# Column mean of an 8192 x 8192 matrix: the loads moved to GpSimd's queue, one packet for each DMA engine, with TensorE announcing the landings

## The chip, the cores and the metric

One core of a Trainium2 chip. The metric is the device time of one execution in microseconds (us). The kernel before takes 627.35 us, the median of three runs (627.28 to 627.52).

The core has a tensor engine (TensorE, PE), a vector engine (VectorE, DVE), a scalar engine (ScalarE, ACT), GpSimd (POOL) and a sync engine (SyncE, SP). Each has its own instruction queue and can issue transfers (DMAs), which 16 DMA engines carry out. Engines tell each other of progress through counting semaphores; a DMA adds 16 to its semaphore when it has landed.

## The reference

```python
x = np.random.randn(8192, 8192).astype(np.float32)

def reference(x):
    return np.mean(x, axis=0)
```

268 MB are read once and 32 KB are written. The work is one addition for each number.

## The kernel before

The matrix has 8192 rows, 64 slabs of 128 rows; a slab fills the 128 partitions of on-chip memory with 32 KiB each. A **pair** is two slabs, 8 MiB (`C` is 8192 columns). 31 pairs (`n_pairs`, k = 0 to 30) are followed by two single slabs. The rows are dealt out so that each of the 128 partitions reads one contiguous run of 64 KiB for a whole pair (`source`, lines 79 to 84; which rows meet in a partition doesn't matter to a sum over all rows).

**Buffers.** There is room for three pairs (`bufs`, line 49). Pair k goes to buffer k % 3, so load k may start only when pair k - 3 has been used up.

**Loads** (lines 123 to 153). `cuts` (86 to 92) says in how many pieces a pair comes. Pair 0 comes in two, 1 MiB and 7 MiB, and both go out on ScalarE's queue. Every other load goes out on SP's queue: pairs 1 to 24 whole, pairs 25 to 29 in two halves, pair 30 in four quarters, then one slab in two halves (key `slab`) and the last slab in eight pieces, the last of them small (key `last`). Load 1 waits for `first`, the landing of the first MiB; load 2 stands behind it and waits for nothing else. From load 3 on, a pair's first piece waits until its buffer is free: for `freed` at least k - 2 while the loop runs, then for a count of VectorE's additions.

**Additions on VectorE.** Line 162 adds the two halves of pair 0 (its own fold). A loop of 8 rounds with 3 pairs each (lines 165 to 173) handles pairs 1 to 24 (`LOOPED`). For each pair it waits for the landing (168), adds the previous pair's running sum to the new pair's first half (169), tells that the previous buffer is free (170, `freed`), and adds the new pair's second half (171). So the sum moves from buffer to buffer, and buffer k - 1 becomes free in the middle of pair k. The semaphore `landed[b]` is reset by the vector engine itself: it subtracts 16 when the pair is consumed. Pairs 25 to 30 and the first slab are added by instructions written out one by one (lines 176 to 182).

**The end.** TensorE first waits until most additions are done (line 223), runs four matmuls that warm it up (225), and then sums over the 128 partitions by matmuls with ones (lines 189 and 201), the total and the last slab's pieces, into eight banks. ScalarE and VectorE scale the banks by 1/8192 (248, 251), and SP and ScalarE store the result (268, 282).

The order of work around the change is written by hand. An engine's queue is worked off in order, so a load that waits holds up the loads behind it on the same queue. Before the change TensorE's queue holds nothing ahead of line 223, and GpSimd's holds no load at all. The lines that matter most:

```python
168  nc.vector.wait_ge(landed[new], 16)
169  vadd(bufs[new][:, 0:C], bufs[old][:, 0:C]).wait_op(landed[old], 0, "sem-eq").then_inc(half, 1)
170  nc.vector.wait_ge(half, n + 1).then_inc(freed, 1)
171  vadd(bufs[new][:, 0:C], bufs[new][:, C : 2 * C]).then_inc(landed[new], -16)
```

Of the kernel before, what the change touches and what calls it, by code (L numbers as in the profile page):

```python
# [20 lines left out]
LOOPED = 24  # L21
# [3 lines left out]
def kernel(  # L25
# [5 lines left out]
    nc = tc.nc  # L31
# [47 lines left out]
    def source(k, lo, hi):  # L79
        if k < n_whole:  # L80
            b, t = divmod(k, RUN // 2)
            return blocks[b, :, 2 * t * C + lo : 2 * t * C + hi]
        j = lo // C
        return single(2 * (k - n_whole) + j, lo - j * C, hi - j * C)

    def cuts(k):
        if k == 0:
            return [(0, FIRST), (FIRST, 2 * C)]
        if k < n_pairs - BY_ROW:
            return [(0, 2 * C)]  # L90
        step = H if k == n_pairs - 1 else C
        return [(lo, lo + step) for lo in range(0, 2 * C, step)]

    with tc.tile_critical():  # L94
        sem = nc.alloc_semaphore
        landed = [sem(f"landed{b}") for b in range(3)]
        first, freed, half = sem("first"), sem("freed"), sem("half")
        dve, act, pe, stored = sem("dve"), sem("act"), sem("pe"), sem("stored")
        came = {}

# [19 lines left out]
            done.append(len(adds))  # L120


        def load(key, dst, src, after=None):

            ld = (nc.scalar if key[0] == 0 else nc.sync).dma_start(out=dst, in_=src)  # L125
            if after is not None:
                ld.wait_op(after[0], after[1], "sem-ge")
            if key not in came:
                came[key] = sem(f"came_{'_'.join(map(str, key))}")
            ld.then_inc(came[key], 16)  # L130

        for k in range(n_pairs):
            for n, (lo, hi) in enumerate(cuts(k)):
                after = None
                if k >= 3 and n == 0:
                    f = k - 3
                    after = (freed, f + 1) if f < LOOPED else (dve, freed_by[f])
                if k == 1:
                    after = (first, 16)
                key = (k, n)  # L140
                if k <= LOOPED:
                    came[key] = first if (k, n) == (0, 0) else landed[k % 3]
                load(key, bufs[k % 3][:, lo:hi], source(k, lo, hi), after)
        r = (n_slabs - 2) * P
        for n in range(2):
            after = (dve, freed_by[n_pairs - 3]) if n == 0 else None
            load(("slab", n), slab[:, n * H : n * H + H], single(n_blocks - 1, n * H, n * H + H), after)
        at, lo = {}, 0
        for n, w in enumerate(PIECES):
            load(("last", n), last[:, lo : lo + w], x[r + P : R, lo : lo + w])  # L150
            for c in range(lo, lo + w, 32):
                at[c] = came["last", n]
            lo += w
# [30 lines left out]


        n_pe = 0

        def mm(dst, src, **flags):
            return nc.tensor.matmul(out=dst, lhsT=ones, rhs=src, skip_group_check=True, **flags)  # L189
# [34 lines left out]
        for _ in range(4):  # L224
            nc.tensor.matmul(  # L225
                out=banks[7][:, 0:512], lhsT=idle[:, 0:P], rhs=idle, start=True, stop=True, skip_group_check=True
# [87 lines left out]
```

## Time and profile before

| | |
|---|---|
| median of three runs | 627.35 us |
| the profiled execution | 627.58 us |
| its span in the profile | 625.8 us |
| VectorE busy | 541.3 us, 86% |
| TensorE busy | 13.7 us, 2% |
| GpSimd busy | 0.2 us, 4 memsets |
| read from main memory | 268.44 MB, 429 GB/s over the span |
| one addition of 128 x 8192 numbers | 8.69 us |
| median of the loop's loads, issue to landing | 29.8 us |

The page cuts the span into 40 slices; for each it gives the busy share of every engine in tenths, the mean busy share of the 16 DMA engines (row "DMA") and the rate of transfer (row "GB/s"). A transfer's bytes are counted where its packet starts, so the rate swings between neighbouring slices where packets are long. The queues are listed with packets and bytes. The chain of waits starts at the last instruction and goes back, at each step, to what released it; a "DMA" in it is the time from a load's issue to its landing, which includes the time that the load spends behind others. The view of a tile's instructions gives the same time for chosen loads.

### The profile page before, as it was taken

To read this page: it belongs to the slowest core of one execution; us is meant where nothing else is said; L and a number is where in the kernel's file an instruction comes from. 1 tells how busy PE (TensorE), PEld (TensorE's weight loads), DVE (VectorE), ACT (ScalarE), POOL (GpSimd) and SP (SyncE) were. 2 spreads that over 40 slices of the span, in tenths; PEclk is the share of its full clock that TensorE was granted. 3 is DMA by queue.
4 is the path that set the end of the run, shared out by engine and by line. 5 is a ranking of instruction groups with operands and counts; after the bars stand their busy time and mean duration, and the time that the engine had idled before them with its cause. 6 is when DMAs were issued, how large, how long until landed. Compare 5 with 4: busy or idle time off the path is not lost.

```text
span 625.8 us, 467 instructions
## 1 busy us (share of the span) xinstructions
PE 13.7 (2%) x86; PEld 4.6 (1%) x86; DVE 541.3 (86%) x71; ACT 3.7 (1%) x6; POOL 0.2 (0%) x4
## 2 busy tenths in 40 slices
PE   0000000000000000000000000000000000000025
PEld 0000000000000000000000000000000000000011
DVE  0049999989888899888898888988889899999996
ACT  0000000000000000000000000000000000000001
POOL 0000000000000000000000000000000000000000
PEclk9999999999999999999999999999999999999999
DMA  9999999999999999999999999999999999999997
GB/s 380 433 461 402 469 402 469 402 469 402 469 402 461 411 452 419 448 423 406 465 402 469 402 469 402 469 402 469 402 469 402 434 429 425 431 425 436 435 429 312
DMA packets 7231, 268.48 MB, mean 429 GB/s; under 512 B 1069, under 2 KB 1329, under 8 KB 1470
## 3 DMA queue, kind: packets, MB, share of 16 engines
q1 hardware_dynamic: 6940, 260.08, 96.1%
q10 hardware_dynamic: 290, 8.39, 3.2%
q14 instruction: 1, 0.01, 0.0%
HBM read 268.44 MB, written 0.03 MB: 429 GB/s over the span
## 4 chain that ended last, share of the span: by engine, by line
DMA 59%; DVE 39%; issue 0%; SPq 0%; PE 0%; DVEq 0%; ACTq 0%
DMA pair<-in_x_dram 59%; DVE pair L157 39%; SPq L125 0%; PE bank L189 0%; DVE row L251 0%; ACTq L125 0%; DVEq L170 0%; DVEq L168 0%; DVEq L157 0%; ACTq L309 0%; SPq L94 0%
## 5 line engine op out<-in xcount | busy, mean ns | idle before, releaser
L157 DVE TENSOR_TENSOR pair<-pair 128x8192 f32<-128x8192 f32 (+1 forms) x32 | 269.6, 8426 | 42.4 <-DMA pair<-in_x_dram 38.7
L157 DVE TENSOR_TENSOR pair<-pair,pair 128x8192 f32<-128x8192 f32 (+2 forms) x35 | 270.1, 7717 | 35.5 <-DMA pair<-in_x_dram 35.0
L225 PE MATMUL bank<-idle 128*128 128x512 f32 x8 | 5.3, 818 | 605.5 <-DVE pair L157 605.5
L189 PE MATMUL bank<-pair,ones 128*32 128x512 f32 (+5 forms) x78 | 8.4, 523 | 3.7 <-DVE pair L157 3.6
L225 PEld LDWEIGHTS bank<-idle 128*128 128x128 f32 x8 | 2.1, 276 | 607.9 <-DVE pair L157 605.5
L248 ACT ACTIVATE rw<-bank 128x512 f32<-128x512 f32 x3 | 1.8, 597 | 617.2 <-PE bank L189 617.2
L251 DVE TENSOR_SCALAR r<-bank 128x352 f32<-128x352 f32 x1 | 0.5, 525 | 3.2 <-PE bank L189 3.2
L189 PEld LDWEIGHTS bank<-pair,ones 128*32 128x32 f32 x78 | 2.6, 108 | 10.2 <-DVE pair L157 7.1
L248 ACT ACT_TABLE_LOAD x1 | 1.3, 1283 | 1.8 <-issue 1.8
L159 DVE MEMSET ones<- 128x32 f32 x1 | 0.1, 85 | 1.0 <-SPq L94 1.0
L248 ACT ACTIVATE row<-bank 1x192 f32<-1x192 f32 (+1 forms) x2 | 0.6, 308 | 0.6 <-PE bank L189 0.6
L160 DVE MEMSET idle<- 128x512 f32 x1 | 0.5, 485 | 0.1
L251 DVE TENSOR_SCALAR row<-bank 1x288 f32<-1x288 f32 x1 | 0.4, 449 | 0.0
L298 POOL MEMSET const-bfloat16-1.0<- 128x1 bf16 x1 | 0.1, 102 | 0.0
L298 POOL MEMSET const-uint8-127<- 128x1 uint8 x1 | 0.1, 102 | 0.0
L298 POOL MEMSET const-float32-0.0<- 128x1 f32 x1 | 0.1, 99 | 0.2 <-issue 0.2
L298 POOL MEMSET const-float32-1.0<- 128x1 f32 x1 | 0.1, 99 | 0.0
## 6 DMA issues: line engine op xcount, KB each, us to landing
pair<-in_x_dram SPq DMA_DIRECT2D x10, 4096.0 KB, 27.6
pair<-in_x_dram SPq DMA_DIRECT2D x6, 2048.0 KB, 28.4
pair<-in_x_dram ACTq DMA_DIRECT2D x1, 7168.0 KB, 38.1
pair<-in_x_dram SPq DMA_DIRECT2D x3, 1024.0 KB, 33.4
pair<-in_x_dram ACTq DMA_DIRECT2D x1, 1024.0 KB, 4.7
pair<-in_x_dram SPq DMA_DIRECT2D x1, 704.0 KB, 36.6
pair<-in_x_dram SPq DMA_DIRECT2D x24, 29.8
pair<-in_x_dram SPq DMA_DIRECT2D x1, 144.0 KB, 30.2
```

The source lines that it names most:

```text
L157: return nc.vector.tensor_tensor(out=a, in0=a, in1=b, op=ADD)
L159: nc.vector.memset(ones, 1.0)
L160: nc.vector.memset(idle, 0.0)
L189: return nc.tensor.matmul(out=dst, lhsT=ones, rhs=src, skip_group_check=True, **flags)
L225: nc.tensor.matmul(out=banks[7][:, 0:512], lhsT=idle[:, 0:P], rhs=idle, start=True, stop=True, skip_group_check=True)
L248: op = engine.mul(out=dst, in_=src, mul=inv_r).then_inc(act, 1)
L251: op = engine.tensor_scalar(out=dst, in0=src, scalar1=inv_r, scalar2=None, op0=MULT).then_inc(dve, 1)
L298: nc = _bacc.Bacc("TRN2", target_bir_lowering=False, num_devices=1)
```

## The change

All loads except pair 0's two pieces go out on GpSimd's queue in place of SP's, with `single_packet=True`: a DMA engine's whole share of a load is framed as one packet. Their waits stay as they were.

The loads of pairs 1 to 24 now add to new semaphores, `count[b]`, one for each buffer, which only ever grow. TensorE waits for each of these 24 landings in turn and adds 16 to `landed[b]`, on which VectorE waits as before. Pair 0's 7 MiB still add to `landed[0]` directly. Pairs 25 to 30, the slab and the last pieces have semaphores of their own, as before. The 24 waits stand on TensorE's queue ahead of line 223.

```diff
+        count = [sem(f"count{b}") for b in range(3)]
...
         def load(key, dst, src, after=None):
-
-            ld = (nc.scalar if key[0] == 0 else nc.sync).dma_start(out=dst, in_=src)
+            if key[0] == 0:
+                ld = nc.scalar.dma_start(out=dst, in_=src)
+            else:
+                ld = nc.gpsimd.dma_start(out=dst, in_=src, single_packet=True)
             if after is not None:
                 ld.wait_op(after[0], after[1], "sem-ge")
...
                 if k <= LOOPED:
-                    came[key] = first if (k, n) == (0, 0) else landed[k % 3]
+                    came[key] = first if (k, n) == (0, 0) else landed[0] if k == 0 else count[k % 3]
                 load(key, bufs[k % 3][:, lo:hi], source(k, lo, hi), after)
...
         n_pe = 0
+        for k in range(1, LOOPED + 1):
+            nc.tensor.wait_ge(count[k % 3], 16 * (k // 3 + (k % 3 > 0))).then_inc(landed[k % 3], 16)
```

## The prediction

> **What bounds the kernel now.** I read the page's slices and queues first, then each load's landing, then the chain of waits at the start, because the change touches only loads and who announces them.
>
> ```profile
> span 625.8 us, 467 instructions
> ...
> DMA  9999999999999999999999999999999999999997
> GB/s 380 433 461 402 469 402 469 402 469 402 469 402 461 411 452 419 448 423 406 465 402 469 402 469 402 469 402 469 402 469 402 434 429 425 431 425 436 435 429 312
> ...
> q1 hardware_dynamic: 6940, 260.08, 96.1%
> q10 hardware_dynamic: 290, 8.39, 3.2%
> ```
>
> The transfer engines are busy in every slice. The swing between 402 and 469 is only the slicing of long packets. q1 is SP's queue and q10 is ScalarE's. ScalarE's two loads are 128 rows each, 256 rows, and its queue shows 290 packets: one packet for each row, and the rest are small entries such as the counts that announce a landing.
>
> The loads of pairs 1, 2 and 3, picked by their time of issue (instructions of the pair buffers in a narrow window; duration in ns, then first and last start in us, then time to landing):
>
> ```profile
> L125 SPq DMA_DIRECT2D pair<-in_x_dram x1: 387/387/387, 5.6 to 5.6; - x1
> ...
> DMA to landing us min/median/max: 36.2/36.2/36.2
> ```
> ```profile
> L125 SPq DMA_DIRECT2D pair<-in_x_dram x1: 411/411/411, 6.1 to 6.1; - x1
> ...
> DMA to landing us min/median/max: 55.1/55.1/55.1
> ```
> ```profile
> L125 SPq DMA_DIRECT2D pair<-in_x_dram x1: 328/328/328, 57.1 to 57.1; - x1
> ...
> DMA to landing us min/median/max: 23.5/23.5/23.5
> ```
>
> So pair 1 lands at 41.8, pair 2 at 61.2, pair 3 at 80.6; by the same view pairs 4, 5 and 6 at 99.8, 119.2 and 138.6. That is (138.6 - 41.8)/5 = 19.36 us for 8 MiB, or 433 GB/s. The fixed cost of a load that finds idle engines comes from the first one: 1 MiB (2.42 us at that rate) lands 4.7 us after its issue, so 2.3 us. Check: 2.3 + 268.44 MB at 433 GB/s (619.5) = 621.8; the last load lands at 621.5. The span is transfer time plus 4.3 us of closing work. VectorE needs 17.5 us a pair against 19.36 and waits. Its unbroken chain from 495 to 582 is no bound either: from its last release, at 582.7, 16 MiB are still to come, 38.7 us at the rate, and they end at 621.5.
>
> A full slice row does not mean that nothing can empty the engines. This is the start, in the chain of waits (start, us, what):
>
> ```profile
> 1.32 38.12 DMA pair<-in_x_dram
> ...
> 39.57 8.70 DVE pair L157
> ...
> 48.29 8.70 DVE pair L157
> ...
> 57.02 0.02 DVEq L170
> ```
>
> Pair 0 is folded at 39.57, pair 1 is added to it at 48.29, and at 57.02 L170 frees buffer 0 for load 3. Load 2 lands at 61.2. With three buffers nothing else can be issued: the engines run dry if buffer 0 comes free more than about 2 us (the fixed cost) after 59.
>
> **How two queues share the engines.** Pair 0's second load is 7 MiB, 16.9 us alone, yet it lands 38.1 us after its issue, when nearly 8 MiB of load 1 have come too. Rows of the two queues took turns, about one each. The queue view of short windows shows it at the end of that load. By 36.5 us all 8.39 MB of q10 have been started; between 36.5 and 38 q10 starts nothing, and between 36.5 and 39.5:
>
> ```profile
> q1 hardware_dynamic: 19, 1.25, 95.7%
> q10 hardware_dynamic: 13, 0.00, 0.2%
> ```
>
> The 13 entries without bytes are 13 of the load's 16 counts. Even a count waited for a whole row of the other queue (64 KiB on one of 16 engines, 2.4 us). A turn is one packet.
>
> **The change, part by part.**
>
> *Framing.* A load of 128 rows is 8 rows for each engine. One packet makes the turn 8 rows, 512 KiB, 19.4 us, in place of 2.4 us. After the start there is one queue only, and nobody to take turns with. At the start there is ScalarE's 7 MiB, 8 rows of 56 KiB for each engine, 2.1 us each. They start about 5 us in, after the first MiB. Load 1 still waits for `first` at 5.6; before, its rows could not come until a fixed cost later, and GpSimd's come about as late or a little later. By then ScalarE has had 2 or 3 rows and needs 5 or 6 and a count. It gets one turn between load 1 and load 2 (two if load 1's count is its own packet), and the remainder only behind load 2. So pair 0 lands last of the three, when all 24 MiB are there: at 61.2, where load 2 landed before (the same bytes, no gap), in place of 39.44.
>
> From there every step has a row. VectorE starts 0.13 later, at 61.3, as it did at 39.57. Buffer 0 is free 17.45 later (57.02 - 39.57), at 78.8. All three buffers are full until then, and the engines idle. Load 3 is issued, finds idle engines, and lands 0.05 + 2.3 + 19.36 later, at 100.5, against 80.6: **+19.9 us**. Does it come back? The engines are the bound, so lost transfer time stays lost. Is there a second gap? Buffer 1 is free at 61.3 + 35.0 = 96.3 and load 3 lands about 101: 4 to 5 us of cover for load 4's start. For load 5 it is 1.8 more (19.36 - 17.5), and so on. No.
>
> *GpSimd in place of SP.* No load of before is issued there, so its price is bounded by rows of the other queues. ScalarE's first load starts its issue at 0.90, and the engines move in the second microsecond; SP spends 0.33 to 0.43 on each. GpSimd may take from 0.4 less than SP to 2.3 more (the whole fixed cost again). I take 0.9 more, near ScalarE's time from issue to motion. It counts once, in load 3's gap: **+0.9**. Load 1's start lies beside ScalarE's 7 MiB. Loads 4 to 24 have 4 to 10.5 us of cover. The last ten loads follow the release at 582.7 with 8 MiB (19.4 us) still ahead of them; up to 3 us each they come in time. What is queued behind a waiting load on GpSimd is only later loads, in the same order as on SP, so nothing else is held up; SP's stores get an empty queue, but their data come after the last landing.
>
> *TensorE's relay.* One semaphore instruction for each of 24 landings, two hops in place of one; VectorE's own such steps (L168, L170) show 0.02 to 0.03 and 0.02 to 0.09 around them, so about 0.1 us. Landing to release of a buffer has 10.5 us of cover in the steady loop, and at pair 3 VectorE is late anyway: nothing. Behind the waits on TensorE stands only the closing work, which waits until 605.5; the last relay is over 100 us earlier. Without cover it would be 24 x 0.1 = 2.4 us.
>
> *Longer packets for the rate.* 19.36 us a load against 8 rows at 2.4 leaves no gap between loads that I can see; a gain by fewer packets is at most some tenths of a per cent, a loss per load anything from nothing to SP's 0.4. I take nothing.
>
> Sum: 19.9 + 0.9 = 20.8 us. Of the profiled execution (span 625.8, 627.58 in all): 646.6 and 648.4. On the median of 627.35: **648.2 us**.
>
> The Trainium skill, DMA: Bandwidth & Descriptors, section "Queues, rings and completion order", says that an engine drains a whole packet of one ring before it goes to another; by it the sum is the same 648. The same page, section "Issuing engines are not separate DMA queues", says that DMAs interleave whichever engine started them and that only issue time changes; by it alone nothing happens, which is the first rival. The one-row turns of before agree with both; no run here yet shows a packet of many rows.
>
> **Rivals.**
>
> *The turns stay short* (0.14), the side that is not slower: the arbiter still changes queue after a row, or the framing is not applied. For it: no row of before shows a long packet. Pair 0 then lands at about 39.5, and load 3 has its 4.2 us (57.0 to 61.2) less the 2.3 for its start: 1.9 us cover GpSimd's 0.9. Time 627.4, from 625.5 to 629. It decides wherever pair 0 lands before about 41.
>
> *Pair 0 gets through between loads 1 and 2* (0.06), because load 1 comes so late that ScalarE has one or two entries left, or turns are weighed by bytes. That needs load 1 to start after about 16 us, 10 after its release. Pair 0 lands at 2.3 + 2 x 19.36 = 41.0, load 3 at about 81.3: +0.7, 628.0. Also within no change.
>
> *VectorE keeps GpSimd from writing* (0.04): each load's release is followed at once by an 8.70 us add. If load 3's issue waits for its end, 8.7 more: 656.9; later loads then have 10.5 - 8.7 = 1.8 us, about enough. The Trainium skill, SBUF — State Buffer, section "Who interferes with whom", has such a lock, but for this add only against GpSimd's reads. No run here shows it yet.
>
> *A gap between packets on top of the forecast* (0.06): up to 0.4 us for each of some 30 loads, 12 us: up to 660.
>
> **Numbers.** The forecast has 0.70. Its own ends: GpSimd's price from -0.4 to +2.3, the start 1 us either way and a slight gain of rate give 645 to 651. The range leaves out the two rivals without change (0.20) and runs from the forecast's low end to 660. A difference under 0.2% (1.25 us) can't be told from no change here. Faster by more: 0.03, all from the first rival. Within: 0.15 (0.09 of the first, 0.06 of the second). Slower: 0.82 (0.70 + 0.04 + 0.06 + 0.02 of the first).
>
> **What would show it.** In the changed trace: pair 0's 7 MiB lands at about 61 in place of 39.4, after loads 1 and 2; VectorE's first add starts there; one or two of the first five slices show engines nearly idle (about 61 to 81), and all others 9; load 3 lands at about 101; from there landings 19.4 apart. If pair 0 lands at 40, framing does not act and the first rival holds; if later slices fall below 9 too, the price is per load; if load 3's issue lies 8.7 after its release, it is VectorE.

## The result and the profile after

The changed kernel takes 630.45 us (median of five runs, 630.34 to 630.59); the kernel before, with the same number of runs, takes 627.52 (627.28 to 627.81). The ratio is 1.0047, 95% interval 1.0033 to 1.0061: slower by 2.9 us, where 20.8 were forecast. The profiled execution took 630.39 us with a span of 628.4.

These lines of the page of the changed kernel answer to those shown of before:

```profile
span 628.4 us, 493 instructions
...
DMA  9999999999999999999999999999999999999995
GB/s 380 430 459 405 463 400 467 400 467 400 467 400 467 400 467 400 467 400 467 400 467 400 467 400 467 400 467 400 467 400 434 434 434 434 434 434 434 434 422 249
...
q0 software_dynamic: 6496, 260.05, 95.7%
```

q0 is GpSimd's queue. No slice shows idle engines, so the gap of the forecast isn't there. The start of the chain of waits shows why (start, us, what):

```profile
1.32 35.66 DMA pair<-in_x_dram
...
37.12 8.70 DVE pair L161
45.84 8.70 DVE pair L161
...
54.68 8.70 DVE pair L161
...
72.44 27.54 DMA pair<-in_x_dram
```

Pair 0's 7 MiB land at 37.0 (before: 39.4), not at 61, and buffer 0 is free at 54.6. By the times to landing (35.9, 54.7, 25.8 and 27.54 us from issues at 5.83, 6.50, 54.88 and 72.44) pairs 1 to 4 land at 41.7, 61.2, 80.7 and 100.0: before's landings within 0.2 us.

The view of the queues shows the turns. When ScalarE's last row starts (window 0 to 32.15 us), so much of load 1 has been started:

```profile
q0 software_dynamic: 80, 5.24, 37.6%
```

That is 80 rows of 64 KiB, 5 for each DMA engine. By the starts in the trace they alternate with ScalarE's last rows one by one: 2.4 us for a row of load 1, 2.1 for one of ScalarE's. In the kernel before it was 96 rows, 6 for each: there load 1's first row started at 9.1 us, here only at 11.1. One row less, 2.4 us, is why pair 0 now lands 2.4 us earlier. At the other end:

```profile
585.62 35.89 DMA pair<-in_x_dram
621.51 0.04 issue
621.55 1.42 PE bank L195 x11
```

621.51 is where before's chain has its last landing too. It is that of the last wide piece, 704 KB; the four narrow pieces land up to 622.5, in both kernels. The last computing instruction, VectorE's at 622.97, starts where it did (622.98). The whole difference in span lies after the work. It is in the view of line 94, which is where the hand-ordered section (`tc.tile_critical`) closes; of before and of after (duration in ns, first and last start in us):

```profile
L94 SPq NOP  x2: 13/13/13, 0.7 to 625.0; - x2
L94 DVEq DRAIN  x1: 10/10/10, 623.6 to 623.6; - x1
L94 PEldq DRAIN  x1: 8/8/8, 623.6 to 623.6; - x1
L94 SPq DRAIN  x1: 407/407/407, 623.6 to 623.6; - x1
...
L94 ACTq DRAIN  x1: 8/8/8, 625.0 to 625.0; - x1
```
```profile
L94 SPq NOP  x2: 13/13/13, 0.7 to 627.6; - x2
L94 POOLq DRAIN  x1: 3986/3986/3986, 623.6 to 623.6; - x1
L94 DVEq DRAIN  x1: 10/10/10, 623.6 to 623.6; - x1
...
L94 ACTq DRAIN  x1: 8/8/8, 625.0 to 625.0; - x1
```

Every engine that took part in the section drains its queue at its end, and SP's NOP marks that all have. Before, ScalarE is last at 625.0, after its wait for the stores. Now GpSimd takes part too, and its drain takes 3986 ns, from 623.55 to 627.54; everything behind it is 2.6 us later. That is the 2.6 us of span. GpSimd has issued its last load by 588.3, but its drain waits, like TensorE's and VectorE's, for a signal that SP gives behind the issue of its last store (622.97 to 623.47 here); in every run these drains begin 0.1 us behind that issue, but for GpSimd's where a drain of its own (below) still runs. SP's own drain takes 0.4 us in both kernels, after 51 transfers issued and after 3. Another 0.2 us lie outside the span (630.39 - 628.4 against 627.58 - 625.8).

### The profile page after: what moved, and what is told of

Same layout as the page of the kernel before. It is cut to its first block, busy times and chain, and to the rows that moved or that the text cites. A ratio compares the mean times of both kernels' runs of the same rounds, so it can differ in the third digit from the quotient of the medians.

```text
span 628.4 us, 493 instructions
## 1 busy us (share of the span) xinstructions
PE 13.7 (2%) x86; PEld 4.6 (1%) x86; DVE 541.2 (86%) x71; ACT 3.7 (1%) x6; POOL 25.6 (4%) x52
## 3 DMA queue, kind: packets, MB, share of 16 engines
q0 software_dynamic: 6496, 260.05, 95.7%
## 4 chain that ended last, share of the span: by engine, by line
DMA 63%; DVE 35%; issue 1%; POOL 0%; PE 0%; PEldq 0%; DVEq 0%; ACTq 0%; SPq 0%
DMA pair<-in_x_dram 63%; DVE pair L161 35%; POOL pair L129 0%; PE bank L195 0%; PEldq L192 0%; DVE row L257 0%; ACTq L127 0%; DVEq L174 0%; DVEq L172 0%; DVEq L161 0%; ACTq L315 0%; SPq L94 0%
## 5 line engine op out<-in xcount | busy, mean ns | idle before, releaser
L129 POOL DMA_DIRECT2D pair<-in_x_dram x48 | 25.4, 532 | 562.4 <-DVEq L174 476.0
## 6 DMA issues: line engine op xcount, KB each, us to landing
pair<-in_x_dram ACTq DMA_DIRECT2D x1, 7168.0 KB, 35.7
pair<-in_x_dram POOLq DMA_DIRECT2D x1, 704.0 KB, 35.9
pair<-in_x_dram POOLq DMA_DIRECT2D x24, 29.4
```

What stands on the lines that cost most here:

```text
L129: ld = nc.gpsimd.dma_start(out=dst, in_=src, single_packet=True)
```

## The experiments

**Theory:** the 2.6 us are GpSimd's drain, and it is long because of the loads that GpSimd issued. **Rivals:** the drain costs 4 us whenever GpSimd takes part; a fixed price for any load; TensorE's relay carries the loss. Beside it stood the question why framing changed nothing in the turns.

**No load on GpSimd, but it takes part** (the kernel before):

```diff
+        nc.gpsimd.wait_ge(first, 16)
```

> The kernel before, with one semaphore wait added on GpSimd inside the section and no load there; nothing of the computation changes. Theory: the changed kernel's 2.6 us of span lie in GpSimd's drain at the section's end (3986 ns, from 623.55), and the drain is long because loads went through GpSimd. Then this drain takes under 0.1 us and the time is before's, 627.3 to 627.8. Rival: every engine that takes part in the section has to drain at its end, and GpSimd's drain takes 4 us whatever it did; then 3.9 to 4.0 us of drain and 630.2 to 630.6.

Measured: ratio 1.000 (0.9989 to 1.001), 627.65 us. The view of line 94:

```profile
L94 POOLq DRAIN  x1: 41/41/41, 624.0 to 624.0; - x1
```

Taking part costs nothing; the loads make the drain long.

**One load on GpSimd:**

```diff
+            elif key[0] != 1:
+                ld = nc.sync.dma_start(out=dst, in_=src)
...
-        for k in range(1, LOOPED + 1):
+        for k in (1,):
             nc.tensor.wait_ge(count[k % 3], ...)
```

> Only load 1 on GpSimd (framed, relayed by TensorE), all others on SP. Theory by number: the drain goes through the loads that GpSimd issued, 3.99 us for 48 or 0.08 each; with one load it takes 0.1 to 0.3 us and ends before ScalarE's wait for the stores, so 627.3 to 627.8. Rival, fixed: the first use of the drain after any GpSimd load costs 4 us (its code is fetched, for example); then 3.9 us and 630.2 to 630.6.

Measured: ratio 1.0269 (1.0248 to 1.0289), 644.5 us, not the time expected, but the drain came out as the theory by number has it:

```profile
L94 POOLq DRAIN  x1: 130/130/130, 640.7 to 640.7; - x1
```

The 17 us are of my making. Load 2 has no wait of its own; it stood behind load 1's wait on one queue. Left on SP, it went out at 0.96 and shared the engines with pair 0 from the start. Pair 0's first MiB, in rows of 8 KiB, took turns with rows of 64 KiB and landed 25.2 us after its issue in place of 4.7, and load 1 went out only at 26.4. Pair 0's second part, which then took turns with load 1, landed at 57.6 (56.2 us after its issue at 1.4), and load 1 last of the three, at 62.3. The table of stretches (us; busy time of PE, PEld, DVE, ACT, POOL; granted clock, DMA share, GB/s, both counted where a packet starts) shows the engines run dry:

```profile
55.00:60.00 5.00, 0.00 (x0) 0.00 (x0) 2.31 (x1) 0.00 (x0) 0.00 (x0) 1.00 0.97 419
60.00:65.00 5.00, 0.00 (x0) 0.00 (x0) 5.00 (x1) 0.00 (x0) 0.00 (x0) 1.00 0.00 0
...
75.00:80.00 5.00, 0.00 (x0) 0.00 (x0) 4.86 (x2) 0.00 (x0) 0.00 (x0) 1.00 1.06 406
```

So the kernel fell by accident into the state that the forecast had described: all buffers full, VectorE starting late (57.69), no transfers for some 14 us, from 62.1 to 76.2. Load 3 goes out at 75.2, and its view ends with:

```profile
DMA to landing us min/median/max: 22.7/22.7/22.7
```

So it lands at 97.9.

**The loop's 24 loads on GpSimd, the later 24 on SP:**

```diff
+            elif key[0] not in range(1, LOOPED + 1):
+                ld = nc.sync.dma_start(out=dst, in_=src)
```

> Loads 1 to 24 on GpSimd, the 24 later ones on SP. Theory by number: half the drain, 1.9 to 2.1 us from 623.55 to 625.6, about 0.6 us past the 624.99 at which before's section ends: 627.9 to 628.4. Fixed: 3.9 us, 630.2 to 630.6.

Measured: ratio 1.0054 (1.0034 to 1.0074), 631.05 us, again not the time expected, but the drain is as the theory by number has it:

```profile
L94 SPq NOP  x2: 13/16/18, 0.7 to 628.7; - x2
L94 POOLq DRAIN  x1: 2016/2016/2016, 626.6 to 626.6; - x1
...
L94 ACTq DRAIN  x1: 8/8/8, 628.0 to 628.0; - x1
```

The drain ends 0.6 us behind ScalarE, as expected, but it begins 3.1 us later than in the changed kernel. Where the loads change queues, load 24 on GpSimd's queue takes turns with load 25 on SP's, and lands 33.0 us after its issue where its predecessor took 29.4. VectorE starts pair 24 late, has no slack from there to the end, and finishes its last addition at 622.57, 3.3 us later than before.

**A drain of its own behind the last load:**

```diff
+        nc.gpsimd.drain()
```

> The changed kernel with a drain of its own on GpSimd, right behind the last load's issue, so that GpSimd waits for its loads there and not at the section's end. Theory by number: the drain goes along with the landings and ends with the last of them, about 621.6 to 622.0; the drain at the section's end finds nothing left, under 0.2 us; time as before, 627.3 to 627.9. Rival, fixed per drain: the last drain takes 4 us again, 630.2 to 630.6. Third: the work on the 48 loads begins only when the last has landed, then it ends about 4 us after 621.9 and the gain is 1.5 us or so, 628.6 to 629.2.

Measured: ratio 1.0004 (0.9994 to 1.0014), 627.91 us, no difference from before. The two drains:

```profile
L160 POOLq DRAIN  x1: 37501/37501/37501, 586.9 to 586.9; - x1
```
```profile
L94 SPq NOP  x2: 13/13/13, 0.7 to 624.9; - x2
...
L94 POOLq DRAIN  x1: 41/41/41, 624.5 to 624.5; - x1
```

The section's own drain is back at 41 ns and the loss is gone, which shows the cause by mending it. The early drain ends at 624.4, 2.0 us after the last landing (622.4) and not with it. That lies between the first expectation and the third: some of its work is done only after the last landing, but it ends ahead of ScalarE (624.9). In what order it goes through the loads stays open.

**More loads, the same bytes:** pairs 25 to 30 cut twice as fine, 62 loads on GpSimd.

```diff
-        step = H if k == n_pairs - 1 else C
+        step = H // 2 if k == n_pairs - 1 else H
```

> The changed kernel with the pieces of pairs 25 to 30 cut in half: 62 loads on GpSimd in place of 48, the same bytes. The drain took 41 ns with no load, 130 with one, 2016 with 24 and 3986 with 48, about 82 for each. By number: 0.04 + 62 x 0.082 = 5.1 us, 1.15 more at the end: 631.5 to 631.8. If the drain goes by bytes or by packets in place of loads (these stay or grow by less than a fifth), 4.0 to 4.4 us and 630.4 to 630.9.

Measured: ratio 1.0097 (1.0067 to 1.0126), 633.52 us.

```profile
L94 POOLq DRAIN  x1: 5129/5129/5129, 626.0 to 626.0; - x1
```

5129 ns against 5.1 us expected: the drain goes by the number of loads, 41 + 82 ns each (one: 130, 24: 2016, 48: 3986, 62: 5129). The time rose by more, because the cut doubled the number of VectorE's additions from pair 25 to 30 (two of 4096 columns take 8.88 us where one of 8192 took 8.70): the drain begins at 626.0 in place of 623.55.

**TensorE's relay alone**, loads on SP:

```diff
-                ld = nc.gpsimd.dma_start(out=dst, in_=src, single_packet=True)
+                ld = nc.sync.dma_start(out=dst, in_=src)
```

> TensorE's relay alone: loads on SP as before, the 24 landings passed on by TensorE. Theory: the relay costs about 0.1 us for each landing, hidden by 10 us of cover, and GpSimd does not take part: 627.4 to 627.9. Rival: the relay carries some of the 2.9 us (24 hops of 0.1 would be 2.4): 629.5 to 630.

Measured: ratio 1.000 (0.999 to 1.0009), 627.56 us. The relay costs nothing that can be measured.

**No framing:**

```diff
-                ld = nc.gpsimd.dma_start(out=dst, in_=src, single_packet=True)
+                ld = nc.gpsimd.dma_start(out=dst, in_=src)
```

> The changed kernel without single_packet, all else equal. Theory: framing acts on nothing here, since a DMA engine turns to another queue after each row of 57 or 64 KB anyway; pair 0's 7 MiB land at 36 to 38 as in the changed kernel (37.0), the drain takes 4.0 us, 630.2 to 630.7. Rival: framing did act, and cost or spared something in the stream; then the landings' spacing (19.32 us) or the time changes by more than 1 us. The last pieces' short rows show whether the flag changes the packets at all: with it the trace has packets of 4608 and 1536 bytes for rows of 768.

Measured: ratio 1.0043 (1.0027 to 1.006), 630.31 us; pair 0's 7 MiB 35.9 us after issue (changed kernel: 35.7), the loop's landings still 19.3 us apart, the drain 3986 ns, and the page has the same 6496 packets on q0. In the trace the last pieces' short rows come in packets of 4608, 3072, 2048 and 1536 bytes, as many of each with the flag as without. In these times and packets the flag leaves no mark.

**Load 1 in pieces of 16 KiB**, framed and not:

```diff
+                ld = nc.gpsimd.dma_start(
+                    out=dst, in_=src, single_packet=key[0] != 1 or True, max_dma_last_dim=16384 if key[0] == 1 else 65536
+                )
```

(The plain run has False in place of True.)

> The changed kernel with load 1's rows cut into four pieces of 16 KiB (32 for each DMA engine, framed as one packet). It asks what a turn is beside ScalarE's 7 MiB. Turn = one piece, framed or not: ScalarE gets 56 KiB against 16, needs about 6 rows and a count from 11 us on, and pair 0 lands at 27 to 30. Turn = 64 KiB or a row: 37 as in the changed kernel. Turn = the framed packet: about 61, and the time rises by 15 to 20 us. In the first two cases the time stays 630 to 631.

> The same cut without framing for load 1. If framing acts, pair 0 lands at another time than in the framed run; if a turn is one piece whatever the framing, both land at 27 to 30.

Measured: 630.49 and 630.34 us, one run of each. Pair 0's 7 MiB, issued at 1.3, in the framed run:

```profile
DMA to landing us min/median/max: 25.1/25.1/25.1
```

and 25.0 in the plain run: it lands at 26.4 and 26.3. When ScalarE's last row starts (window 0 to 23.45 us), the framed run has started this much of load 1:

```profile
q0 software_dynamic: 80, 1.31, 13.0%
```

It is 80 again, as in the changed kernel, but pieces of 16 KiB; the plain run has the same 80 and 1.31 MB. ScalarE gets 56 KiB for each 16 KiB of GpSimd's. A turn is one piece, with the flag and without. Expected were 27 to 30, so even that is a little late by my count.

**What a load costs that finds idle engines**, from SP and from GpSimd (`gap_sp` from the kernel before, `gap_pool` from the changed one):

```diff
-FIRST = 2048
+FIRST = 16128
```

> The kernel before with pair 0 cut at 16128 in place of 2048 columns, so that load 1, which waits for the first piece, finds the engines idle but for 128 KiB (0.3 us). It measures what a load costs that finds idle engines, from SP. By the fixed 2.3 us of the prediction: the first piece lands at 22.2, load 1 at 22.3 + 2.3 + 19.4 = 44.0 (before 41.8), all later landings 2.1 later, 629.6 to 629.9.

> The same cut in the changed kernel, so that load 1 finds idle engines from GpSimd. The prediction took GpSimd's start as 0.9 us dearer than SP's (bounds -0.4 and +2.3): load 1 lands at 44.9, 0.9 after that of the SP run, and the time is 630.45 + 3.0 = 633.4. If GpSimd's start costs the same, 632.5.

Measured: 630.78 us, ratio 1.0056 (1.0033 to 1.0079), from SP; 634.04 us, 1.0105 (1.0076 to 1.0135), from GpSimd. The starts in the chains of waits, SP's and then GpSimd's, each with the times to landing of loads 1 and 2 (the shortest is load 1's):

```profile
0.90 21.98 DMA pair<-in_x_dram
...
22.89 0.39 SPq L125
```
```profile
DMA to landing us min/median/max: 22.6/32.1/41.5
```
```profile
0.91 21.84 DMA pair<-in_x_dram
...
23.05 0.66 POOL pair L129
```
```profile
DMA to landing us min/median/max: 22.3/31.7/41.1
```

Load 1 lands 22.6 us after its issue at 22.89 from SP and 22.3 after 23.05 from GpSimd; from the first piece's landing (22.88 and 22.75) it is 22.6 us in both. GpSimd's first rows do start later, 1.7 us after that landing against SP's 1.0, but the load lands no later; why stays open. So GpSimd's start costs the same as SP's, and the last wide pieces land together in these two kernels (625.15 and 625.14). Of the 3.3 us between their times 2.6 are the drain again and 0.2 to 0.3 lie outside the span; the rest is scatter of the runs (the two profiled ones are 2.8 apart). The cost of a start is 22.6 - 19.36 = 3.2 us, not 2.3.

## Why the prediction was wrong

**The step that failed** is *Framing*: "One packet makes the turn 8 rows, 512 KiB, 19.4 us, in place of 2.4 us." The runs showed that a turn stays one piece, 64 KiB or 16 KiB, with the flag and without: 5 pieces of load 1 for each engine came between ScalarE's 8 rows, and pair 0 landed at 37.0, not at 61.2. So load 3 met no gap, and of the 19.9 us nothing was left. The count itself was right (ScalarE has had 3 rows when load 1's first starts, and needs 5 more); the size of a turn was not. I had read "a turn is one packet" from rows in which packet, row and piece are the same thing; that "framed as one packet" moves the border of a turn was only argued. Of the two rules weighed beside it, the Trainium skill's "Issuing engines are not separate DMA queues" (DMA: Bandwidth & Descriptors) held for the stream: the landings of pairs 1 to 4 are before's within 0.2 us. The Trainium skill's rule of whole packets (same page, "Queues, rings and completion order") is not contradicted if a packet is what the trace records as one, but no run here made a packet of several long pieces.

**What followed from it was right.** If pair 0 lands late, the engines idle until VectorE has freed buffer 0. In the run with one load on GpSimd pair 0 lands at 57.6; the prediction's steps then give load 3 at 57.6 + 0.13 + 17.45 + 0.05 + a start + 19.36, with the measured start of 3.2 at 97.8. It landed at 97.9, 17.3 later than 80.6, and that run's span is 643.0, 17.2 over before's. The condition was false, not the chain.

**The rival that came true has its price wrong.** The first rival (turns stay short, chance 0.14) names the right mechanism and gives 627.4. Only pair 0 it puts at 39.5 in place of 37.0, and its 1.9 us of cover for load 3 would have been 1.0 with a start of 3.2; with buffer 0 free at 54.6 it is 3.4. What it lacks, as does the forecast, is the end, a second step that failed: "The span is transfer time plus 4.3 us of closing work" was carried over unchanged, though GpSimd was added to the engines that the section drains, and it became 6.9 (628.4 - 621.5). Part of the closing is not in the kernel's text but follows from which engines take part. The view of line 94 of before would have shown the place: TensorE's, VectorE's, SP's and ScalarE's drains, none of GpSimd. It could not have shown the price, 82 ns for each load.

**The other terms.** GpSimd in place of SP: taken as +0.9 us at a start, measured 0 at the landing. The relay: nothing, as said. No gain and no loss for the rate, as said. VectorE's additions don't hold GpSimd up: its issues start 0.3 us after each release and take 0.53 us while VectorE adds, as the Trainium skill (SBUF — State Buffer, "Who interferes with whom") has it for additions of this kind. The 0.2 us outside the span were not foreseen. The runs with 48 loads on GpSimd have 2.0 to 2.2 us outside, all others, the one with 62 among them, 1.7 to 1.8; its cause stays open.

## What to carry to other kernels

When a stream is bound by its transfers, moving it to another queue changes little in the stream; look at what the new engine adds at the start and at the end, and which engines take part in a section's closing. GpSimd's drain costs 82 ns for each load that it has issued and not yet drained, so few large loads there, or a drain of its own behind the last load, well ahead of the section's end; even so it only got back to the old time here. And read the wait of a load as its queue gives it: a load without a wait of its own may live on the wait of the one ahead of it.

## What the runs showed of the hardware

- GpSimd's drain: 41 ns with no load issued, then 82 ns for each load, whatever its size (130, 2016, 3986 and 5129 ns for 1, 24, 48 and 62). SP's drain stays at 0.4 us with 51 transfers issued or with 3.
- Two queues take turns by piece: 16 KiB against 56 KiB let the 7 MiB land at 26.4 us, 64 KiB against 56 KiB at 37.0, and 8 KiB against 64 KiB stretched the landing of 1 MiB from 4.7 to 25.2 us after its issue. The queue with the smaller pieces loses.
- A load from GpSimd takes 0.53 us of its time, but from the release to the landing an 8 MiB load is as fast as one from SP (22.6 us on idle engines).
- Short rows travel one by one from SP and in packets of up to 4608 bytes from GpSimd: packets under 2 KB fell from 1329 to 833. The last landing did not move (622.5).
